# A kernel of two hybrid trunk layers on one core: S5 chunk states laid out by group instead of by chunk

## The chip, the cores and the metric

The kernel runs on one core of a Trainium2 chip. The metric is the time of one execution in microseconds (us) on the device. The engines of the core are named as in the profile: PE is the tensor engine's matmuls and PEld its weight loads (they overlap), DVE is VectorE, ACT is ScalarE, POOL is GpSimd, SP is the engine that issues nearly all DMAs.

## The reference, cut to what matters

Two layers run over 640 tokens (512 of a denoising request, 128 of a prompt) with 1024 channels. Each layer has a gated linear attention branch, a latent attention branch and an S5 branch, joined by gates. The change is in the S5 branch, a diagonal complex state space model over 32 groups with 64 states each, run forwards and backwards:

```
def complex_linear_scan(ab_re, ab_im, u_re, u_im, x0_re, x0_im):
    u_re = u_re.at[:, 0].add(ab_re * x0_re - ab_im * x0_im)
    u_im = u_im.at[:, 0].add(ab_re * x0_im + ab_im * x0_re)
    ...
    _, _, x_re, x_im = lax.associative_scan(combine, (a_re, a_im, u_re, u_im), axis=1)
    return x_re, x_im
...
    finals.append(jnp.stack([x_re[:, -1], x_im[:, -1]], axis=1))
    ...
    y_ssm = jnp.einsum('blgn,gpn->blgp', x_re, c_re) - jnp.einsum('blgn,gpn->blgp', x_im, c_im)
```

So for every group a state is carried from token to token (once in each direction), the output is a product of the states with a matrix per group, and the states after the prompt are themselves an output (`new_state_s5`).

## The kernel before, in words

The kernel cuts the 640 tokens into 80 chunks of 8. Per chunk and group it keeps one state per direction; the 128 partitions hold the 64 states' real and imaginary parts. These chunk states are X, one tile (named `mx` in the profile) of 128 partitions by 5248 elements of 4 bytes, with 164 chunk places times 32 groups: places 0 to 80 for the forward direction (`XZ[0]`), 82 to 161 for the backward one (`XZ[1]`), place 80 and 81 for the final states. Before the change the group is the last axis: the 32 groups of one chunk are neighbours, and the same group of the next chunk is 32 elements, 128 bytes, further.

Three stages of a layer work on X.

- `s5_z` (line 829) fills it: PE multiplies the chunk inputs `U` with a matrix per group and direction into PSUM, and ACT copies four groups by 80 chunks at a time into X (32 copies in all, through the helper on line 229).
- `s5_scan` (line 900) runs the recurrence on DVE. Fifteen steps treat 5 blocks of 16 chunks in both directions at once, 2 x 5 x 32 = 320 elements: five instructions each (lines 916 to 920), of which each reads or writes X once. Four single steps of 2 x 32 elements join the blocks. Then the DMAs of the final states leave (lines 930, 931). In a last part, for three blocks and two directions, four instructions of 15 x 32 = 480 elements (lines 951 to 954) add what came in from the block before; 951, 953 and 954 touch X, 952 takes a copy with changed sign that line 938 has made (96 elements).
- `s5_y` (line 957) makes the output on PE: for each group three matmuls with 80 columns of stationary operand, one with `U` (chunks are neighbours in it) and two with X (lines 972 to 975). A matmul of 4-byte operands shows as two pairs of weight load and matmul in the trace, so a group is six pairs. All matmuls are recorded under the helper's line 247.

What stands between these stages on PE is written out by hand: `fill(n)` takes n parts of projections that are wanted anyway. Each of the 24 turns of the scan is followed by `fill(4)`. A part is a contraction step of 128 channels, six pairs of load and matmul (four with the weight's rounded part `whi`, two with the rest `wlo`). Four parts share one half of a weight tile: SP loads it (`wraw`, line 268), ACT rounds it (`whi`, line 229), DVE subtracts (`wlo`, line 238), and each of the three has four buffers. The order on PE is the order of the program; on the other engines a scheduler sets a fixed order at build time, with the splits put between the scan's instructions.

Of the kernel before, what the change touches and what calls it, by code (L numbers as in the profile page):

```python
# [10 lines left out]
F32 = mybir.dt.float32  # L11
# [12 lines left out]
NC8 = 80  # L24
NB = 16
# [178 lines left out]
class Prog:  # L204
# [624 lines left out]
    def s5_z(self, p, fill):  # L829
        V = self.V  # L830

        X = self.mx().rearrange("p (c g) -> p c g", g=32)
        XZ = (X[:, 0:81], X[:, 82:162])
        sh = [128, 4, 8, 16]
        def front(b, d):
            r = p.tile([128, 4, 8, 16], F32, name="s5r", tag=f"s5r{d}", bufs=2 + d)
            tmp = p.tile([128, 4, 8, 16], F32, name="s5rtmp", tag=f"s5rtmp{d}", bufs=1)
            g = slice(32 * d + 4 * b, 32 * d + 4 * b + 4)
            w = [self.w[:, :, i, g].rearrange("p e g -> p g e") for i in range(2)]
            if d == 0:  # L840
                w = [x[:, :, ::-1] for x in w]
            self.outer(V, p, r, tmp, w[0], w[1], self.B1[:, 4 * b:4 * b + 4], self.B2[:, 4 * b:4 * b + 4], sh)
            ps = self.bank()
            for i in range(4):
                self.T.transpose(ps[:, 128 * i:128 * i + 128], r[:, i].rearrange("p a b -> p (a b)"), self.ident)
            pm = p.tile([128, 512], F32, name="s5pm", tag="s5pm", bufs=3)
            self.copy(pm, ps)
            return pm

        def back(b, d, pm):  # L850
            pz = self.bank()
            for i in range(4):
                self.mm(pz[:, NC8 * i:NC8 * i + NC8], pm[:, 128 * i:128 * i + 128], self.U[:, 4 * b + i, :])
            z = pz[:, 0:4 * NC8].rearrange("p (g c) -> p c g", g=4)
            gs = slice(4 * b, 4 * b + 4)
            if d == 0:
                self.copy(XZ[0][:, 1:81, gs], z)
            else:
                self.copy(XZ[1][:, 0:79, gs], z[:, 1:80])

        todo = []
        for n in range(16):
            todo.append((n // 2, n % 2, front(n // 2, n % 2)))
            if n:
                back(*todo.pop(0))
            fill(FILL[2])
        back(*todo.pop(0))
        x0 = self.vec("x0")
        V.tensor_copy(X[:, 81, :], XZ[1][:, 63, :])
        V.tensor_copy(XZ[0][:, 0, :], x0[:, 0:32])  # L870
        V.tensor_copy(XZ[1][:, 63, :], x0[:, 32:64])
        V.memset(XZ[0][:, 64, :], 0.0)
        V.memset(XZ[1][:, 79, :], 0.0)
        self.X, self.XZ = X, XZ

# [24 lines left out]
    def s5_scan(self, p):  # L900

        V = self.V
        X = self.X
        pt = self.pt.rearrange("p r e (d g) -> p r e d g", d=2)

        def at(f, b, n=1):

            a = X[:, f:82 + b + 1:82 + b - f, :]
            ps, ds, gs = a.ap
            return bass.AP(tensor=a.tensor, offset=a.offset, ap=[ps, ds, [NB * 32, n], gs])  # L910

        def step(prev, cur, e, n):
            ar, ai = (pt[:, r, e][:, :, None, :].to_broadcast([128, 2, n, 32]) for r in range(2))
            t1 = p.tile([128, 2, n, 32], F32, name="sc1", tag="sc1", bufs=2)
            t2 = p.tile([128, 2, n, 32], F32, name="sc2", tag="sc2", bufs=2)
            V.tensor_tensor(t1, prev, ar, op=ALU.mult)
            V.tensor_tensor(t2[0:64], prev[64:128], ai[64:128], op=ALU.mult)
            V.tensor_tensor(t2[64:128], prev[0:64], ai[0:64], op=ALU.mult)
            V.tensor_tensor(t1, t1, cur, op=ALU.add)
            V.tensor_tensor(cur, t1, t2, op=ALU.add)  # L920

        for i in range(1, NB):
            step(at(i - 1, NB - i, 5), at(i, NB - 1 - i, 5), 0, 5)
            yield
        step(at(79, 64), at(80, -1), 0, 1)
        for k in range(1, 4):
            step(at(NB * k - 1, 64 - NB * k), at(NB * k + NB - 1, 48 - NB * k), NB - 1, 1)
            yield
        o = self.o["s5o"][self.l]
        self.S.dma_start(o[:, 0:32], X[:, 80, :])  # L930
        self.S.dma_start(o[:, 32:64], X[:, 81, :])
        n = NB - 1
        sh = [128, n, 32]
        sw = p.tile([128, 2, 3, 32], F32, name="s5sw")
        for d in range(2):
            c = X[:, 15:48:16] if d == 0 else X[:, 98:131:16]
            for a, b in ((slice(0, 64), slice(64, 128)), (slice(64, 128), slice(0, 64))):
                V.tensor_scalar(sw[a, d], c[b], -1.0, None, op0=ALU.mult)
        for k in range(3):
            for d in range(2):  # L940
                t1 = p.tile(sh, F32, name="sf1", tag="sf1", bufs=2)
                t2 = p.tile(sh, F32, name="sf2", tag="sf2", bufs=2)
                if d == 0:
                    c = X[:, NB * k + 15]
                    x = X[:, NB * k + 16:NB * k + 16 + n]
                    w = [pt[:, r, 0:n, d] for r in range(2)]
                else:
                    c = X[:, 82 + NB * (k + 1)]
                    x = X[:, 82 + NB * k + 1:82 + NB * k + 16]
                    w = [pt[:, r, 0:n, d][:, ::-1] for r in range(2)]  # L950
                V.tensor_tensor(t1, w[0], c[:, None, :].to_broadcast(sh), op=ALU.mult)
                V.tensor_tensor(t2, w[1], sw[:, d, k][:, None, :].to_broadcast(sh), op=ALU.mult)
                V.tensor_tensor(x, x, t1, op=ALU.add)
                V.tensor_tensor(x, x, t2, op=ALU.add)
                yield
# [531 lines left out]
    def fill(self, n):  # L1487

        for _ in range(n):
            while self.stand:  # L1490
                try:
                    next(self.stand[0])
                    break
                except StopIteration:
                    self.stand.pop(0)
# [187 lines left out]
```

## Time and profile before

| | |
|---|---|
| median of 3 runs | 1574.49 us (1572.39 to 1583.06) |
| the profiled execution | 1574.24 us, span 1572.5 us |
| PE busy | 1506.5 us, 96% |
| DVE busy | 1054.3 us, 67% |
| ACT busy | 629.5 us, 40% |
| DMA, over the span | 182.09 MB, mean 116 GB/s |
| the 256 X pairs of `s5_y` | 46.1 us of matmul, 302 ns each (overlapping) |

The span is the time from the first to the last recorded instruction of the profiled execution. Busy time is what an engine spent in instructions; matmuls overlap, so that the distance of their starts says more than their duration. A row of a timeline gives the start, the time from the first start to the last end, the engine, line, operation, output and input with their shapes, and how many instructions in a row were merged. A row of grouped instructions gives after the bar the total in us and the mean in ns of one, and behind it the idle time ahead of them.

### The profile page before, as it was taken

The page shows a single profiled execution, that of the slowest core. Times are in us where ns is not written, and L with a number is a line of the kernel's source. Part 1 is how long each engine was busy: PE and PEld are TensorE (multiplying, and loading weights), DVE is VectorE, ACT ScalarE, POOL GpSimd, SP SyncE. Part 2 cuts the span into 40 slices and gives each one's busy share as a digit, 9 for nine tenths or more (in the row PEclk, how much of TensorE's full clock was granted, in tenths as well). Part 3 has the DMA queues.
Part 4 walks back from the last instruction along what each step waited for, and adds up shares of the span by engine and source line. Part 5 has one row for each costly group of instructions (what it writes and reads, how often), then busy time and mean ns, then how long its engine had stood idle before and what let it go on. Part 6 is the DMA issues. An engine that isn't in the chain of part 4 may idle for free. (4 is left out here: it accounts for less than half of the span.)

```text
span 1572.5 us, 28798 instructions
## 1 busy us (share of the span) xinstructions
PE 1506.5 (96%) x11334; PEld 1436.7 (91%) x11334; DVE 1054.3 (67%) x2435; ACT 629.5 (40%) x1171; POOL 46.5 (3%) x48
## 2 busy tenths in 40 slices
PE   5998999999999999999999899999999999999998
PEld 3788999988999888898998899999999999888998
DVE  8979694796556536879577579645766563487662
ACT  3324323555444454322324442254544442633321
POOL 0000000011000000000000000001300000000000
PEclk9998999999999999999999999999999999999999
DMA  9451435243312221237753333442331223212253
GB/s 347 158 151 49 122 113 167 90 133 102 103 63 75 85 75 56 78 110 241 258 195 99 97 79 113 138 133 87 115 114 61 74 81 111 69 55 68 91 169 104
DMA packets 109656, 182.09 MB, mean 116 GB/s; under 512 B 12752, under 2 KB 31120, under 8 KB 109520
## 3 DMA queue, kind: packets, MB, share of 16 engines
q1 hardware_dynamic: 109520, 180.25, 36.3%
q8 instruction: 89, 1.46, 0.4%
q14 instruction: 47, 0.39, 0.1%
HBM read 150.41 MB, written 29.79 MB: 115 GB/s over the span
## 5 line engine op out<-in xcount | busy, mean ns | idle before, releaser
L247 PE MATMUL pj<-h,whi 128*128 128x320 f32 x3456 | 664.8, 314 | 0.2 <-DVE og L488 0.2
L247 PEld LDWEIGHTS pj<-h,whi 128*128 128x128 f32 x3456 | 541.7, 189 | 6.5 <-issue 5.1
L229 ACT ACTIVATE whi<-wraw 128x512 fp32r<-128x512 f32 x326 | 204.9, 630 | 517.3 <-PE pj L247 384.1
L247 PE MATMUL pj<-h,wlo 128*128 128x320 f32 x1728 | 397.6, 310 | 0.0
L238 DVE TENSOR_TENSOR wlo<-wraw,whi 128x512 fp32r<-128x512 f32 x326 | 223.9, 688 | 216.5 <-ACT whi L229 209.8
L247 PEld LDWEIGHTS pj<-h,wlo 128*128 128x128 f32 x1728 | 290.8, 189 | 0.0
L247 PE MATMUL pj<-og,whi 128*128 128x320 f32 x736 | 142.9, 314 | 2.4 <-DVE og L238 2.4
L247 PEld LDWEIGHTS pj<-og,whi 128*128 128x128 f32 x736 | 115.4, 189 | 6.9 <-DVE og L238 3.2
L247 PE MATMUL pj<-whi,h 128*128 128x512 f32 x256 | 86.6, 400 | 5.1 <-ACT h L232 4.4
L247 PE MATMUL pj<-og,wlo 128*128 128x320 f32 x384 | 87.8, 310 | 0.0
L247 PEld LDWEIGHTS pj<-whi,h 128*128 128x128 f32 x256 | 48.8, 192 | 17.4 <-ACT h L232 5.0
L247 PEld LDWEIGHTS pj<-og,wlo 128*128 128x128 f32 x384 | 64.5, 188 | 0.0
L232 ACT ACTIVATE P<-bank,smx 128x384 f32<-128x384 f32 x64 | 36.5, 576 | 49.8 <-DVE smx L1235 49.8
L238 DVE TENSOR_TENSOR Ptl<-bank,Pth 128x512 fp32r<-128x512 f32 x48 | 31.7, 687 | 31.1 <-ACT Pth L229 30.9
L232 ACT ACTIVATE th<-pj 128x640 f32<-128x640 f32 x72 | 49.7, 690 | 6.3 <-PE pj L247 6.2
L247 PE MATMUL pj<-wlo,h 128*128 128x512 f32 x128 | 50.6, 396 | 0.0
L247 PE MATMUL pj<-s5g,whi 128*128 128x320 f32 x256 | 48.1, 310 | 0.0
L247 PE MATMUL bank<-s5qy,mx 128*80 128x128 f32 x256 | 46.1, 302 | 0.0
L577 DVE SCALAR_TENSOR_TENSOR mx<-pj,ada,tmp 128x320 f32<-128x320 f32 (+2 forms) x48 | 18.1, 433 | 39.6 <-PE pj L247 37.5
L1231 DVE TENSOR_REDUCE smx<-bank 128x1 f32<-128x384 f32 (+1 forms) x72 | 36.5, 524 | 10.6 <-PE bank L247 10.0
L229 ACT ACTIVATE Pth<-bank 128x512 fp32r<-128x512 f32 x48 | 27.1, 596 | 35.3 <-PE bank L1256 35.3
L1421 DVE SCALAR_TENSOR_TENSOR st<-st,bl,bank 64x128 f32<-64x128 f32 x112 | 38.8, 347 | 3.5
(349 smaller groups left out, 2320.2 us busy)
## 6 DMA issues: line engine op xcount, KB each, us to landing
wraw<-wpk SPq DMA_DIRECT2D x358, 256.0 KB, 2.8
og<-wpk SPq DMA_DIRECT2D x48, 256.0 KB, 5.4
qd<-s5qk SPq DMA_DIRECT2D x32, 256.0 KB, 2.9
s5qy<-qd SPq DMA_DIRECT2D x32, 256.0 KB, 4.0
gd<-gt SPq DMA_DIRECT2D x16, 320.0 KB, 2.8
gt<-gd SPq DMA_DIRECT2D x16, 320.0 KB, 3.1
md<-th SPq DMA_DIRECT2D x16, 320.0 KB, 2.3
th<-md SPq DMA_DIRECT2D x16, 320.0 KB, 3.5
```

Source lines behind the costliest of these rows:

```text
L229: self.A.activation(out, in_, AF.Copy, scale=scale)
L232: self.A.activation(out, in_, f, **kw)
L238: (eng or self.V).tensor_tensor(lo, src, hi.bitcast(F32), op=ALU.subtract)
L247: self.T.matmul(out, lhsT, rhs, start=start, stop=stop, skip_group_check=True, **kw)
L577: V.scalar_tensor_tensor(xn[:, j, lo:hi], ps[:, i, lo - 320 * i:hi - 320 * i], self.ads[l, 2][r][:, j:j + 1], xr[:, lo:hi], op0=ALU.mult, ...
L1231: V.tensor_reduce(mx[:, i:i + 1], ps[:, 0:w], axis=AX.X, op=ALU.max)
L1421: V.scalar_tensor_tensor(out, st[r, c, :], bl[r, c:c + 1], pu[c][r], op0=ALU.mult, op1=ALU.add)
```

## The change

X is laid out the other way round: the group is the outer axis and the 164 chunk places of a group are neighbours. The same chunk of the next group is 164 elements, 656 bytes, further. ACT's copies in `s5_z` go over groups outside and chunks inside. The scan keeps its order of dimensions (chunks outside, 32 groups inside). The final states are first copied into a small tile, and one DMA of 64 elements per partition takes the place of two of 32.

```diff
@@ s5_z
-        X = self.mx().rearrange("p (c g) -> p c g", g=32)
+        X = self.mx().rearrange("p (g c) -> p c g", g=32)
...
-            z = pz[:, 0:4 * NC8].rearrange("p (g c) -> p c g", g=4)
+            z = pz[:, 0:4 * NC8].rearrange("p (g c) -> p g c", g=4)
             gs = slice(4 * b, 4 * b + 4)
             if d == 0:
-                self.copy(XZ[0][:, 1:81, gs], z)
+                self.copy(XZ[0][:, 1:81, gs].rearrange("p c g -> p g c"), z)
             else:
-                self.copy(XZ[1][:, 0:79, gs], z[:, 1:80])
+                self.copy(XZ[1][:, 0:79, gs].rearrange("p c g -> p g c"), z[:, :, 1:80])
@@ s5_scan
-            return bass.AP(tensor=a.tensor, offset=a.offset, ap=[ps, ds, [NB * 32, n], gs])
+            return bass.AP(tensor=a.tensor, offset=a.offset, ap=[ps, ds, [NB, n], gs])
...
         o = self.o["s5o"][self.l]
-        self.S.dma_start(o[:, 0:32], X[:, 80, :])
-        self.S.dma_start(o[:, 32:64], X[:, 81, :])
+        xe = p.tile([128, 2, 32], F32, name="s5xe")
+        V.tensor_copy(xe, X[:, 80:82, :])
+        self.S.dma_start(o, xe.rearrange("p d g -> p (d g)"))
```

On DVE the order of the instructions stays. This is the place in layer 0 where the four single steps meet the last part of the scan (`sc` and `sf` are the scan's temporaries, `s5pt` the powers of the transition, `wlo` a weight split, `gt` a gate); - is before, + is the change:

```order
@@ -432,11 +432,12 @@
 L919 TENSOR_TENSOR sc_2542<-sc_2542,mx 128x64
 L918 TENSOR_TENSOR sc_2550<-mx,s5pt 64x64
-L951 TENSOR_TENSOR sf_2672<-s5pt,mx 128x480
+L952 TENSOR_TENSOR sf_2673<-s5pt,mx 128x480
 L238 TENSOR_TENSOR wlo<-wraw,whi 128x512
 L919 TENSOR_TENSOR sc_2549<-sc_2549,mx 128x64
-L920 TENSOR_TENSOR mx<-sc_2542,sc_2543 128x64
+L920 TENSOR_TENSOR mx<-sc_2542,sc_2543 128x2x32
 L488 SCALAR_TENSOR_TENSOR gt<-th,pj 128x640
-L953 TENSOR_TENSOR mx<-mx,sf_2672 128x480
+L954 TENSOR_TENSOR mx<-mx,sf_2673 128x15x32
 L920 TENSOR_TENSOR mx<-sc_2549,sc_2550 128x2x32
+L931 COPY s5xe<-mx 128x64
 L238 TENSOR_TENSOR wlo<-wraw,whi 128x512
```

Only the copy is new; the shapes show that the 480 elements of X are no longer one run, and the lines behind the new one have moved by one.

On SP's queue this is the place of the final states in layer 0 (`gd` is a store of a gate, `wraw` a raw weight load); first before:

```order
70 L1062 DMA gd_104<-gt 128x640
71 L268 DMA wraw<-wpk 128x512 x2
72 L930 DMA s5o<-mx 128x32
73 L931 DMA s5o<-mx 128x32
74 L1062 DMA gd_104<-gt 128x640
75 L268 DMA wraw<-wpk 128x512 x2
```

and with the change:

```order
70 L1063 DMA gd_104<-gt 128x640
71 L268 DMA wraw<-wpk 128x512 x2
72 L1063 DMA gd_104<-gt 128x640
73 L932 DMA s5o<-s5xe 128x64
74 L268 DMA wraw<-wpk 128x512 x2
75 L1063 DMA gd_104<-gt 128x640
```

The one DMA that is left stands behind one gate store more than the two did. PE's and ACT's order is unchanged, and so is the order of everything else on DVE and SP, but that in layer 1 the one DMA of final states also stands one place from where the two did.

## Rows read from the trace of the kernel before

**Rows 1.** Page, busy us by engine, share of the span, instructions.

```profile
PE 1506.5 (96%) x11334; PEld 1436.7 (91%) x11334; DVE 1054.3 (67%) x2435; ACT 629.5 (40%) x1171; POOL 46.5 (3%) x48
```

**Rows 2.** Stretches: length, busy us (instructions) by engine, PE clock, DMA share, GB/s.

```profile
170.00:246.10 76.10, 76.10 (x521) 76.05 (x520) 73.50 (x154) 20.01 (x32) 0.00 (x0) 1.00 0.44 134
...
931.00:1004.20 73.20, 73.20 (x501) 73.20 (x500) 70.64 (x151) 19.58 (x32) 0.00 (x0) 1.00 0.42 126
```

**Rows 3.** Timeline of PE in s5_y, layer 0: start, us, what.

```profile
254.71 0.38 PE L247 MATMUL bank<-s5m,s5u 128*80 128x128 f32 x2
254.93 0.72 PE L247 MATMUL bank<-s5qy,mx 128*80 128x128 f32 x4
255.49 0.38 PE L247 MATMUL bank<-s5m,s5u 128*80 128x128 f32 x2
255.70 0.72 PE L247 MATMUL bank<-s5qy,mx 128*80 128x128 f32 x4
...
260.14 0.38 PE L247 MATMUL bank<-s5m,s5u 128*80 128x128 f32 x2
...
261.80 0.75 PE L984 MATMUL bank<-c,s5yb 80*128 80x80 f32 x8
262.34 0.83 PE L247 MATMUL pj<-h,whi 128*128 128x320 f32 x4
```

**Rows 4.** Groups of DVE instructions by shape: total us, mean ns; idle before.

```profile
L549 DVE TENSOR_TENSOR mx<-mx,tmp 128x640 f32<-128x640 f32 x32 | 26.2, 818 | 0.1
...
L916 DVE TENSOR_TENSOR sc<-mx,s5pt 128x320 f32<-128x320 f32 x30 | 14.7, 490 | 0.9
...
L920 DVE TENSOR_TENSOR mx<-sc,sc 128x320 f32<-128x320 f32 x30 | 14.7, 489 | 0.6
...
L954 DVE TENSOR_TENSOR mx<-mx,sf 128x480 f32<-128x480 f32 x12 | 7.6, 649 | 0.0
...
L938 DVE TENSOR_SCALAR s5sw<-mx 64x96 f32<-64x96 f32 x8 | 2.0, 248 | 0.1
...
L916 DVE TENSOR_TENSOR sc<-mx,s5pt 128x64 f32<-128x64 f32 x8 | 1.8, 222 | 0.1
```

**Rows 5.** Groups of ACT instructions by shape, as above.

```profile
L229 ACT ACTIVATE mx<-bank 128x320 f32<-128x320 f32 x16 | 7.0, 438 | 4.1 <-PE bank L247 4.1
...
L229 ACT ACTIVATE s5u<-bank 128x320 f32<-128x320 f32 x16 | 6.1, 432 | 4.0 <-PE bank L824 4.0
```

**Rows 6.** Timeline of ACT, the last halves rounded in layer 0's scan.

```profile
243.18 0.63 ACT L229 ACTIVATE whi<-wraw 128x512 fp32r<-128x512 f32 x1 [2.30 <-PE pj L247]
```

**Rows 7.** Timeline of DVE, the end of the scan in layer 0.

```profile
244.81 1.22 DVE L954 TENSOR_TENSOR mx<-mx,sf 128x480 f32<-128x480 f32 x2
245.94 0.68 DVE L238 TENSOR_TENSOR wlo<-wraw,whi 128x512 fp32r<-128x512 f32 x1
```

**Rows 8.** Timeline of PE, the last projections ahead of s5_y, layer 0.

```profile
253.83 0.75 PE L247 MATMUL pj<-h,whi 128*128 128x320 f32 x4
254.42 0.46 PE L247 MATMUL pj<-h,wlo 128*128 128x320 f32 x2
```

**Rows 9.** Timeline of DVE, the end of the scan in layer 1.

```profile
1002.95 0.68 DVE L238 TENSOR_TENSOR wlo<-wraw,whi 128x512 fp32r<-128x512 f32 x1
1003.55 0.64 DVE L954 TENSOR_TENSOR mx<-mx,sf 128x480 f32<-128x480 f32 x1
```

**Rows 10.** Timeline of PE, projections ahead of s5_y, layer 1.

```profile
1012.14 0.46 PE L247 MATMUL pj<-h,wlo 128*128 128x320 f32 x2
```

**Rows 11.** Stretches ahead of and in s5_z, layer 0, columns as in rows 2.

```profile
120.00:130.00 10.00, 4.57 (x38) 4.07 (x36) 7.10 (x13) 4.59 (x9) 0.00 (x0) 0.80 0.35 111
130.00:140.00 10.00, 8.31 (x50) 8.29 (x51) 10.00 (x18) 2.66 (x5) 0.00 (x0) 0.68 0.01 2
```

**Rows 12.** Timeline of PE there, behind a wait for DVE.

```profile
132.43 1.42 PE L247 MATMUL pj<-h,whi 128*128 128x320 f32 x4
...
134.18 1.05 PE L845 MATMUL bank<-c,s5r 128*128 128x128 f32 x4
```

## Prediction

> **What bounds the kernel now.** I began with busy time by engine: the tensor engine (PE) is busy for 96% of the span, VectorE (DVE) for 67% [rows 1]. A microsecond taken from PE's own work is therefore nearly a microsecond of the run, and DVE work costs nothing as long as PE doesn't wait for it. But 67% is a mean over stages, so the next view is busy time by stretch, around the lines that the diff touches. The S5 scan runs at 170 to 246 us in layer 0 and at 931 to 1004 us in layer 1, and in both DVE is busy for 96.6% of the time (73.50 of 76.10 us, 70.64 of 73.20 us) while PE is never idle [rows 2]. PE works there on projections (the `fill` calls), whose weights DVE has to split, in the same queue as the scan's instructions. So there are two full engines side by side, and the change touches both: it shortens something on PE in the output stage that follows (`s5_y`), and it changes the address pattern of almost everything that DVE does in the scan.
>
> **What it gives PE.** In `s5_y` a group of channels takes six pairs of weight load and matmul: two with the input `U` as stationary operand, four with the chunk states X. Each pair has 128 moving columns and a stationary operand of 80 columns. The two U pairs take 0.22 or 0.21 us together, so 0.1075 us a pair; from group to group it is (260.14 - 254.71) / 7 = 0.776 us [rows 3]. The four X pairs thus take 0.56 us, 0.140 us a pair. The only difference between the operands is the step from column to column: 4 bytes in U, 128 bytes in X. After the change X has 4 bytes too, so I give its pairs U's price: six pairs of 0.1075 us are 0.645 us, and 0.131 us is saved per group. With 32 groups in each of two layers that is 64 x 0.131 = **8.4 us off PE**. The lower bound is nothing, if the extra 0.03 us a pair is not the load's; U's pairs, of the same shape, speak against that. PE's order of instructions is the same as before, so nothing else moves there.
>
> **What it costs DVE.** The neighbours in X are now the chunks, but the scan still runs over 32 groups inside and chunks outside, so each of its accesses to X has an innermost step of 164 elements, 656 bytes, where it had 4 bytes. The elements touched in a layer: in the 15 steps, five instructions of 320 (L916 to L920, 30 each in two layers); in the four single steps, five of 64; in the last part 18 of 480 (L951, L953 and L954, 12 each in two layers; L952 doesn't touch X); and the sign flips, four of 96 [rows 4]. That is 24,000 + 1,280 + 8,640 + 384; with five small fills and copies of 32 and the new copy of 64, 34,528 elements.
>
> No DVE instruction of before reads or writes with such a step, so its price has to be bounded. Below: nothing. ScalarE's copies into X read PSUM with a step of 320 bytes and take 438 ns, against 432 ns for the copy of as many elements into U, which reads neighbours [rows 5]. So a long step can be free, on another engine and from PSUM. The nearest row for the same memory is PE's: a column 128 bytes from the last one costs 0.140 us / 80 = 1.75 ns, while eight loads of 128 neighbouring columns with their transposes take 262.34 - 261.80 = 0.54 us, at most 0.53 ns a column [rows 3]. DVE needs (818 - 490) ns / 320 = 1.025 ns per neighbouring element (640 against 320 elements) [rows 4]. If an element on a line of its own takes DVE as long as PE, the extra is 0.725 ns; if DVE needs a second beat, which is what an engine with a beat of 1.025 ns does when 1.75 ns don't fit into one, it is 1.025 ns. I take the second beat, since the scan's memory is the one of PE's row and not that of ScalarE's, and keep 0 and 0.725 ns for the range.
>
> [...]
>
> With the second beat a layer's scan grows by 34,528 x 1.025 ns = 35.4 us, and the new copy adds about 0.2 us at its old price (a 64-element instruction takes 222 ns [rows 4]): **E = 35.6 us per layer**.
>
> **How much of E is hidden.** DVE's order is also the same as before, apart from the new copy in either layer: the weight splits (`wlo`) stand between the same scan instructions. DVE has no idle time that could take E, so a split late in the stage comes later by all of it. What hides is PE's lead. Four buffers of split weights go round; one half lasts PE four times the 0.88 us between 253.83 [rows 8] and 254.71 [rows 3], 3.52 us, and the half whose first part is written at 243.18 [rows 6] is used three halves later, at 253.83. Its `wlo` is ready at 245.94 + 0.68 = 246.62 [rows 7] and wanted at 254.42 [rows 8]: a lead of 7.8 us. The scan itself ends at 244.81 + 1.22 = 246.03 [rows 7], and the first X pair is at 254.93 [rows 3], a lead of 8.9 us; the split decides. In layer 1 the last split inside the scan ends at 1003.63, ahead of the scan's last instruction (0.64 us, of which about 0.5 us is its share of E) [rows 9], and is wanted at 1012.14 [rows 10]: 8.5 + 0.5 = 9.0 us. So PE waits (35.6 - 7.8) + (35.6 - 9.0) = 27.8 + 26.6 = **54.4 us**. The waits can't be made up, because PE has no idle time afterwards in which it would have been waiting for something else.
>
> The edits left: ScalarE's 32 copies into X now write neighbours and read neighbours; by [rows 5] that is at most 6 ns each, off the path. On SP's queue two DMAs of final states become one, which waits for the new DVE copy; behind it stand gate stores and weight loads. The copy sits right behind the instruction for which the old DMAs waited, so the wait is the copy's own 0.3 us or so, and the four raw weight buffers cover it; if they didn't, PE would wait 0.3 us per layer. I count nothing.
>
> **The sum.** Against the profiled run's own 1574.24 us (span 1572.5 us and 1.7 us around it; the median of the runs shown is 1574.49 us): 1574.24 - 8.4 + 54.4 = 1620.2 us. The change breaks even where 2E - 16.8 = 8.4 us, that is E = 12.6 us, an extra of 0.36 ns per element.
>
> **The rivals.**
> *The step is dearer for PE than free, but less than a second beat.* With 0.725 ns, E = 25.2 us, the waits are 33.6 us, the time is 1599.4 us. If reads pay the second beat and writes are free (L920 and the small writes, some 5,100 elements, drop out), E = 30.4 us and the time is 1609.8 us. [...]
> *The step is free for DVE.* Then E is the new copy's 0.2 us, far under the 7.8 us of lead; PE waits for nothing, and the time is 1574.24 - 8.4 = 1565.8 us. This is the case on the other side; it decides for every extra under 0.36 ns an element. ScalarE's copies speak for it, PE's loads against.
> *Dearer still.* L953 and L954 read and write X in one instruction; if both ends pay apart, 12 x 480 x 1.025 ns = 5.9 us more per layer gives 1632 us. [...]
> *The change doesn't do what it says:* X's loads stay dear for another reason, and the scan slows all the same: 1628 us.
>
> **How the numbers follow.** Second beat 0.48; between free and second beat, 0.20; dearer still 0.10; loads unchanged 0.04; free 0.18. The likeliest gives **1620 us**. The range from 1592 to 1645 us takes in everything but "free" and a far tail, so about 8 in 10. A measurement here tells about 1% from no change, 16 us: "free" (0.5% faster) is within it. Slower by over 1%: 0.80; within 1%: 0.18; faster by over 1%: 0.02, for which PE would have to gain twice what its rows allow.
>
> **What would show it.** Right: L916 to L920 at about 490 + 328 = 820 ns for 320 elements and L954 at about 1,140 ns; PE waiting for `wlo` or X inside the scan stages, some 27 us in each; X pairs in `s5_y` at U's 0.1075 us. Wrong: scan instructions still at 490 ns with PE at 100% through the scan, and a span shorter by 8 us. Slow scan instructions without waits of PE would mean that I misjudged the lead.

## The result and the profile after

The changed kernel takes 1616.86 us (median of six runs, 1614.26 to 1619.62) against 1574.82 us for the kernel before, measured beside it: a ratio of 1.0258, with a 95% interval of 1.0232 to 1.0285. The profiled execution took 1619.62 us, 1617.8 us of it span. The forecast was 1620.0 us in a range of 1592 to 1645 us, "slower" with 0.80. So the time is as forecast; but two terms of the sum, the length of the scan and the part of it that is hidden, are wrong by a quarter and more, and their errors cancel.

Busy time by engine on the page after (columns as in [rows 1]), and the two scan stages (as in [rows 2]; the stretches hold the DVE instructions of those of before and the new copy):

```profile
PE 1517.0 (94%) x11334; PEld 1444.3 (89%) x11334; DVE 1107.0 (68%) x2437; ACT 630.0 (39%) x1171; POOL 46.4 (3%) x48
```

```profile
169.18:271.97 102.79, 87.43 (x537) 85.83 (x537) 100.19 (x155) 21.25 (x34) 0.00 (x0) 0.90 0.33 102
955.89:1055.30 99.41, 82.06 (x526) 80.10 (x525) 96.88 (x152) 20.18 (x33) 0.00 (x0) 0.93 0.31 93
```

VectorE (DVE) gained 52.7 us of busy time, all of it in these two stages (26.7 and 26.2 us): they last 102.8 and 99.4 us where they lasted 76.1 and 73.2 us, and DVE is busy for 97% of them. The tensor engine (PE), which never paused there, is idle for 102.79 - 87.43 = 15.4 us in layer 0, and its pairs of load and matmul take 87.43 us / 537 = 0.163 us each in place of 76.10 us / 521 = 0.146 us, at a mean granted clock of 0.90.

The groups of DVE instructions by shape that answer to [rows 4] (line 955 is line 954 of before, 939 is 938; line 953, which doesn't touch X, is there for comparison):

```profile
L920 DVE TENSOR_TENSOR mx<-sc,sc 128x320 f32<-128x320 f32 x30 | 22.4, 745 | 0.6
L916 DVE TENSOR_TENSOR sc<-mx,s5pt 128x320 f32<-128x320 f32 x30 | 22.2, 741 | 0.9
L955 DVE TENSOR_TENSOR mx<-mx,sf 128x480 f32<-128x480 f32 x12 | 12.5, 1060 | 0.0
L953 DVE TENSOR_TENSOR sf<-s5pt,s5sw 128x480 f32<-128x480 f32 x12 | 7.8, 669 | 0.0
L939 DVE TENSOR_SCALAR s5sw<-mx 64x96 f32<-64x96 f32 x8 | 2.6, 323 | 0.1
L916 DVE TENSOR_TENSOR sc<-mx,s5pt 128x64 f32<-128x64 f32 x8 | 2.2, 269 | 0.1
```

320 elements went from 490 to 741 or 745 ns, that is 0.79 ns more per element; 480 elements from 649 to 1060 ns, 0.86 ns; 64 from 222 to 269 ns, 0.73 ns; 96 from 248 to 323 ns, 0.78 ns. With the numbers of elements of the prediction: 24,000 x 0.79 + 8,640 x 0.86 + 1,280 x 0.73 + 384 x 0.78 ns + 0.2 us = 27.8 us per layer, not 35.6 us. Neighbouring instructions overlap a little (the L955 that starts at 263.02 us lasts 1.07 us, and the next instruction starts at 263.96 us), so the distance says more: from the start of its first instruction to the end of its last, the scan takes 102.4 us in place of 75.7 us in layer 0 and 98.7 us in place of 72.5 us in layer 1, that is 26.7 and 26.2 us more, as DVE's busy time has it.

What PE waited for, in all (us in total, times, longest; the list goes on with waits that were there before):

```profile
PE pj L247 <- DVE misc L1056: 15.7, 2, 9.0
PE pj L247 <- DVE gt L488: 14.4, 9, 3.7
...
PE pj L247 <- DVE wlo L238: 3.0, 3, 1.3
```

33 us of new waits, and only 3 us of them for the weight splits (`wlo`) that the prediction named. The others are for lines 488 and 1056. These are DVE's evacuations, the instructions that empty a `pj` tile: the gate (`gt`), and an addition into `misc`. PE writes its projections into two `pj` tiles in PSUM in turn, so a projection can't start before DVE has read out the last but one.

S5_y, the timeline of PE in layer 0 (start, us, what; answers to [rows 3]):

```profile
278.12 0.38 PE L247 MATMUL bank<-s5m,s5u 128*80 128x128 f32 x2
278.34 0.60 PE L247 MATMUL bank<-s5qy,mx 128*80 128x128 f32 x4
...
282.71 0.38 PE L247 MATMUL bank<-s5m,s5u 128*80 128x128 f32 x2
```

Seven groups take 282.71 - 278.12 = 4.59 us, 0.656 us each in place of 0.776 us. The first X pair stands at 278.34 us, 23.4 us later than before; as this scan began 0.8 us earlier, 24.2 us were lost from the scan's start to s5_y. In layer 1 the same stretch (from the scan's first instruction, 931.66 before and 956.55 after, to the first X pair, 1016.17 and 1064.37) grew by 23.3 us. The s5_y stages, from the first X pair to the end of the last, got shorter by 3.5 and 3.9 us. 24.2 + 23.3 - 7.4 = 40.1 us of the 45.3 us between the two spans. Of the other 5 us, 1.5 us in each layer are matmuls behind s5_y at a lower clock (0.62 as the mean of 326 to 330 us in layer 0). This spell comes and goes from one execution to the next: of the runs below five have it in one layer and the others in none, with waits in the scan or without. The last 2 us lie scattered between the stages, where the run with the states alone (below) differs from before by 3.6 us with no change there.

### The profile page after: what moved, and what is told of

Read it like the earlier page. It is cut to its first block, busy times and chain, and to the rows that moved or that the text cites. A ratio compares the mean times of both kernels' runs of the same rounds, so it can differ in the third digit from the quotient of the medians.

```text
span 1617.8 us, 28792 instructions
## 1 busy us (share of the span) xinstructions
PE 1517.0 (94%) x11334; PEld 1444.3 (89%) x11334; DVE 1107.0 (68%) x2437; ACT 630.0 (39%) x1171; POOL 46.4 (3%) x48
## 5 line engine op out<-in xcount | busy, mean ns | idle before, releaser
L247 PE MATMUL pj<-h,whi 128*128 128x320 f32 x3456 | 675.8, 317 | 30.3 <-DVE misc L1056 15.7
L247 PEld LDWEIGHTS pj<-h,whi 128*128 128x128 f32 x3456 | 550.5, 192 | 39.7 <-issue 34.9
L247 PE MATMUL pj<-h,wlo 128*128 128x320 f32 x1728 | 402.1, 313 | 3.0 <-DVE wlo L238 3.0
L247 PEld LDWEIGHTS pj<-h,wlo 128*128 128x128 f32 x1728 | 294.8, 191 | 3.8 <-DVE wlo L238 3.8
L247 PEld LDWEIGHTS pj<-whi,h 128*128 128x128 f32 x256 | 48.7, 191 | 18.6 <-ACT h L232 6.3
L247 PEld LDWEIGHTS pj<-s5g,whi 128*128 128x128 f32 x256 | 42.2, 197 | 0.0
```

Of the source, the lines that this page charges most:

```text
L247: self.T.matmul(out, lhsT, rhs, start=start, stop=stop, skip_group_check=True, **kw)
```

## The fixed order, seen between two gates

DVE's timeline from one gate to the next, before:

```profile
208.13 0.82 DVE L488 SCALAR_TENSOR_TENSOR gt<-th,pj 128x640 f32<-128x640 f32 x1
...
210.92 0.69 DVE L238 TENSOR_TENSOR wlo<-wraw,whi 128x512 fp32r<-128x512 f32 x1
...
215.12 0.82 DVE L488 SCALAR_TENSOR_TENSOR gt<-th,pj 128x640 f32<-128x640 f32 x1
```

and after:

```profile
221.93 0.81 DVE L488 SCALAR_TENSOR_TENSOR gt<-th,pj 128x640 f32<-128x640 f32 x1
...
225.74 0.69 DVE L238 TENSOR_TENSOR wlo<-wraw,whi 128x512 fp32r<-128x512 f32 x1
...
231.47 0.81 DVE L488 SCALAR_TENSOR_TENSOR gt<-th,pj 128x640 f32<-128x640 f32 x1
```

In both there are ten scan instructions, two splits and the gate, in the same order. Before, this takes 215.12 - 208.13 = 6.99 us. One projection takes PE eight times 0.88 us, 7.04 us: here the order fits PE's pace exactly and leaves no slack. After, it takes 231.47 - 221.93 = 9.54 us, 2.55 us more, and the next projection but one has to wait for it. The longest wait is for the first such evacuation, which has 39 scan instructions ahead of it since the scan's start in layer 0 (63 in layer 1, where the wait is 9.0 us). Layer 0, DVE, then PE; the bracket is the wait:

```profile
202.46 0.82 DVE L1056 TENSOR_TENSOR misc<-pj,misc 32x640 fp32r<-32x640 f32 x1
```

```profile
203.43 1.40 PE L247 MATMUL pj<-h,whi 128*128 128x320 f32 x4 [6.68 <-DVE misc L1056]
...
205.16 1.27 PE L247 MATMUL pj<-h,whi 128*128 128x320 f32 x4
```

After 6.68 us without work the next six pairs take 205.16 - 203.43 = 1.73 us in place of 0.88 us: the granted clock is 0.52 as the mean of 200 to 210 us. That is why the sum of the waits is smaller than the loss: the rest is PE working slowly, ahead of its next wait.

## The experiments

Ratios are to the kernel before, run beside each of them, with 95% intervals.

**A price list.** Behind the last layer of the kernel before, such lines as

```diff
+    V.tensor_tensor(d(), src[:, 0:1280:4], C, op=ALU.mult)  # read step 4
+    V.tensor_tensor(W[:, 0:10, :], X[:, 0:10, :], C3, op=ALU.mult)  # read and write step 164
```

> The kernel before, and behind its last layer a list of single operations that belong to no result: fp32 multiplications and copies of 320 elements per partition on VectorE with the elements of one operand 1, 2, 3, 4, 8, 16 or 164 floats apart (read, written, or both), copies of 640 elements on ScalarE with a step of 32 floats on either side, two operations on GpSimd, and groups of 16 matmuls whose 80-column stationary operand is 1 to 64 floats apart. It asks whether the step alone is what made the scan's instructions longer (490 to 741 ns for 320 elements). Theory (the step alone): about 490 ns at step 1 and about 740 ns at step 164, for a read as for a write and for both together, and a bend at some step between; a matmul pair that gets shorter from step 32 to step 1 by about 79 + 29 ns, as in the changed kernel. Rival (the scan's own surroundings made it longer, by ScalarE or PE using the same memory at that time): 490 ns at every step when nothing else runs. Rival (each strided operand costs by itself): 740 ns for one strided operand, about 990 ns for two. The total time says nothing here but that some 50 us stand behind the last layer.

DVE's groups (lines 1667 to 1673: read steps of 1, 2, 3, 4, 8, 16 and 164 floats; 1674: pairs of neighbours, eight floats from pair to pair; 1675 to 1678: writes with steps of 2, 4, 16 and 164; 1679: one read and the write with 164; 1680: both reads):

```profile
L1667 DVE TENSOR_TENSOR pdst<-mx,pcon 128x320 f32<-128x320 f32 x1 | 0.5, 484 | 0.0
L1668 DVE TENSOR_TENSOR pdst<-mx,pcon 128x320 f32<-128x320 f32 x1 | 0.5, 485 | 0.0
L1669 DVE TENSOR_TENSOR pdst<-mx,pcon 128x320 f32<-128x320 f32 x1 | 0.6, 581 | 0.0
L1670 DVE TENSOR_TENSOR pdst<-mx,pcon 128x320 f32<-128x320 f32 x1 | 0.7, 721 | 0.0
...
L1673 DVE TENSOR_TENSOR pdst<-mx,pcon 128x320 f32<-128x320 f32 x1 | 0.7, 720 | 0.0
L1674 DVE TENSOR_TENSOR pdst<-mx,pcon 128x320 f32<-128x320 f32 x1 | 0.5, 497 | 0.0
L1675 DVE TENSOR_TENSOR pwide<-pcon 128x320 f32<-128x320 f32 x1 | 0.5, 486 | 0.0
...
L1678 DVE TENSOR_TENSOR pwide<-pcon 128x320 f32<-128x320 f32 x1 | 0.7, 747 | 0.0
L1679 DVE TENSOR_TENSOR pwide<-mx,pcon 128x320 f32<-128x320 f32 x1 | 0.8, 751 | 0.0
L1680 DVE TENSOR_TENSOR pdst<-mx 128x320 f32<-128x320 f32 x1 | 0.7, 735 | 0.0
```

The step alone does it, with no scan around it. The cost bends between 2 floats (485 ns, free) and 4 (721 ns), and stays there up to 164 (720 ns). A write pays as a read does (747 and 720 ns at 164 floats), and two strided operands cost no more than one (735 and 751 ns): that rival is out. So is the surroundings' share: ScalarE did nothing meanwhile, and PE's loads, which ran beside the whole list, ran beside the steps of 1 and 2 floats too. In bytes of the step it is 485 ns at 8, 581 ns at 12 and 721 ns at 16; what sets the place of the bend no run shows.

PE's weight loads in the same list, with steps of 1, 2, 4 and 32 floats (each row from a stretch inside the 32 loads of that step):

```profile
L247 PEld LDWEIGHTS bank<-pcon,mx 128*80 128x80 f32 x11 | 1.2, 150 | 0.0
L247 PEld LDWEIGHTS bank<-pcon,mx 128*80 128x80 f32 x23 | 2.6, 153 | 0.0
L247 PEld LDWEIGHTS bank<-pcon,mx 128*80 128x80 f32 x29 | 4.3, 243 | 0.0
L247 PEld LDWEIGHTS bank<-pcon,mx 128*80 128x80 f32 x26 | 3.7, 233 | 0.0
```

So PE's loads bend at the same place: 8 bytes are nearly free (153 against 150 ns), 16 bytes have the whole price (243 ns, against 233 ns at 128 bytes).

**PE's side alone.** S5_y loads 80 neighbours of X, which are other states than those that the reference takes there; the amount of work is the same, and the scan is that of before:

```diff
-                    self.mm(o, self.XZ[d][:, 0:NC8, g], q[d][:, i],
+                    self.mm(o, self.flat[:, 162 * g + 81 * d:162 * g + 81 * d + NC8], q[d][:, i],
```

> The kernel before, whose s5_y loads 80 neighbouring columns of X for each of its 64 groups in place of 80 columns 128 bytes apart: the matrix that it takes is another one than the reference's (other states), the number of matmuls, loads, columns and waits is the same. Only TensorE's side of the change is in it. Theory: the two s5_y stages get shorter by 3.5 and 3.9 us, the sum 7.4 us, so 1574.2 - 7.4 = about 1567 us, a ratio of 0.995, and the group at 0.65 to 0.66 us. The prediction's own term says -8.4 us, 1566 us. Rival (the shorter group came from VectorE or ScalarE, which are less in its way in the changed kernel): no change, 1574.

Measured: 0.9951 (0.9935 to 0.9966), 7.7 us off. All 256 X matmuls have the changed kernel's 273 ns, where before has 302 ns. The gain is the load's.

```profile
L247 PE MATMUL bank<-s5qy,mx 128*80 128x128 f32 x256 | 38.4, 273 | 0.0
```

**The final states alone.**

```diff
-        self.S.dma_start(o[:, 0:32], X[:, 80, :])
-        self.S.dma_start(o[:, 32:64], X[:, 81, :])
+        xe = p.tile([128, 2, 32], F32, name="s5xe")
+        V.tensor_copy(xe, X[:, 80:82, :])
+        self.S.dma_start(o, xe.rearrange("p d g -> p (d g)"))
```

> The kernel before with one part of the change alone: the two final states are copied into a small tile by VectorE and written out by one transfer in place of two. X keeps its layout. Theory: one copy of 64 elements (0.1 to 0.2 us) in each layer on VectorE, one DMA issue less on SyncE, and nobody waits for either: 1575 us, a ratio of 0.999 to 1.001. Rival (the copy or the later issue is what costs some of the 42 us): a ratio over 1.002.

Measured: 0.9994 (0.9980 to 1.0008). This part costs nothing that can be measured.

**VectorE's length alone, in the layout of before.** Only the scan's scratch tiles are strided (and have one buffer in place of two, by which the last part of the scan gets another order on DVE):

```diff
-            t1 = p.tile([128, 2, n, 32], F32, name="sc1", tag="sc1", bufs=2)
+            t1, t2 = (p.tile([128, 2, n, 32, 4], F32, name=f"sc{i}", tag=f"sc{i}", bufs=1)[:, :, :, :, 0] for i in (1, 2))
```

> The kernel before with X laid out as before (groups as neighbours, TensorE's loads 128 bytes apart as before), in which only the scan's scratch tiles (sc1, sc2, sf1, sf2) have their elements four floats apart. The price list gave 712 to 741 ns for a 320-element multiplication with one operand four floats apart, and 735 to 751 ns with two, against 484 ns with none. TensorE's order of instructions is that of before. Theory (the length of the scan's instructions on VectorE is all that counts, wherever it comes from; X's layout itself is innocent): the scan's own instructions take 27 to 28 us more in each layer as in the changed kernel, TensorE waits some 24 us in each layer in the lines of the gate and misc, and the time is 1574 + 47 to 52 = 1621 to 1626 us, a ratio of 1.030 to 1.033. Rival (X with a step of 656 bytes is what disturbs TensorE or ScalarE): VectorE's instructions longer, but clearly less than +40 us. Rival (the prediction's lead of 7.8 and 9.0 us): 1574 + 38 = 1612 us.

Measured: 1.0308 (1.0294 to 1.0322). DVE's groups (its lines 919 and 952 are 920 and 954 of before) and PE's waits:

```profile
L919 DVE TENSOR_TENSOR mx<-sc,sc 128x320 f32<-128x320 f32 x30 | 22.0, 734 | 0.6
...
L952 DVE TENSOR_TENSOR mx<-mx,sf 128x480 f32<-128x480 f32 x12 | 12.3, 1023 | 0.2
```

```profile
PE pj L247 <- DVE misc L1053: 15.5, 2, 9.1
PE pj L247 <- DVE gt L488: 15.1, 10, 3.4
```

X is untouched, PE's order is that of before, and the loss is the changed kernel's with the same two waits: 22.3 and 24.4 us from the scan's start to s5_y, against 24.2 and 23.3 us. The sum closes too: the changed kernel's 1.0258 and the 0.0049 that PE's side gave make 1.0307, and this run has 1.0308. That it is so close is partly chance, since these scans grew by 28.1 and 28.9 us (all four instructions of the last part are strided here).

**The same length, made of more instructions.** Scan instructions are done twice, all with neighbours:

```diff
+            if n > 1:
+                V.tensor_tensor(t1, prev, ar, op=ALU.mult)
+                V.tensor_tensor(t2[0:64], prev[64:128], ai[64:128], op=ALU.mult)
```

> The kernel before, with its layout and neighbouring accesses, in which some of the scan's multiplications are done twice into the same tile with the same values: about 26.5 us more of VectorE in each of the two scans, spread along it as the changed kernel's longer instructions are. Nothing is strided and TensorE's loads stay. Theory (VectorE's time alone makes the wait, through the tiles in PSUM that it must empty, and only 2 to 3 us of it in each layer are hidden): TensorE waits for the gate and misc lines of VectorE, 23 to 25 us in each layer with the slower clock, about 1574.2 + 48 = 1622 us. The prediction's lead (7.8 and 9.0 us, by the weight splits): 1574.2 + 53 - 16.8 = about 1610 us, and waits on the tile wlo. Rival (the strided accesses disturb the other engines, and the time of VectorE is not what counts): far less than +40 us.

Measured: 1.0247 (1.0219 to 1.0274), +39 us: between the two sums. PE's timeline at s5_y says why:

```profile
274.69 1.29 PE L247 MATMUL bank<-s5qy,mx 128*80 128x128 f32 x4 [16.98 <-DVE mx L961]
```

The order of DVE was made anew for the added instructions: from the second one on, most evacuations still have 9 to 16 scan instructions ahead of them, and 32 stand behind the last gate. So PE does all its projections at its own pace and then waits once, 17 us, for X. DVE's busy time grew by 25.1 us a layer, and s5_y began 19.9 and 19.4 us later after the scan's start, so 5 to 6 us are hidden in each layer. S5_y itself begins at a granted clock of 0.50 (274.7 to 278.7 us), and is 2.1 and 2.3 us longer than before. The time of DVE alone makes a wait, but its place and part of its size come from the order. How much less the changed kernel would lose in such an order was not measured: no run has its accesses in another order, and none gives PE a third `pj` tile.

**Evacuations first.**

```diff
-        self.V.scalar_tensor_tensor(self.v2(g), self.v2(th), 1.0, ps, op0=ALU.add, op1=ALU.mult)
+        with self.tc.high_priority(4000):
+            self.V.scalar_tensor_tensor(self.v2(g), self.v2(th), 1.0, ps, op0=ALU.add, op1=ALU.mult)
```

> The changed kernel, in which VectorE's instructions that empty TensorE's two PSUM tiles (the gate of line 488 and the addition of line 1056) are given a higher priority, so that they stand further ahead in VectorE's order. The work is the same. Theory (TensorE's wait comes through these two tiles, and only 2 to 3 us per layer are hidden by them): the waits on the gate and misc lines shrink, those on the weight split (wlo) take their place, and the lead grows towards the 7.8 and 9.0 us that the prediction read off the splits: up to 6 us per layer less than the changed kernel, so 1605 to 1612 us against 1617. Rival (the prediction: the weight split is what TensorE waits for): no change, 1617 us, since the splits come no earlier. Rival (VectorE's time in the scan is simply longer than TensorE's work, whatever the order within it): no change in the sum either, with the wait moved to another line.

Measured: 1.0244 (1.0218 to 1.0269). The raised priority moved no instruction on PE, DVE or ScalarE, so this is a second measurement of the changed kernel and tells nothing of the order.

**More standing work in the scan.** `FILL[3]`, the number of parts of projections (units) behind each turn of the scan, is 5 and 6 in place of 4:

```diff
-FILL = (17, 2, 1, 4, 1, 4, 10, 1, 7, 1)
+FILL = (17, 2, 1, 5, 1, 4, 10, 1, 7, 1)
```

> The changed kernel, in which the scan's stage is given five units of standing work after each step of the scan in place of four: about 24 units more for TensorE in each layer, taken from the stages behind it. Theory (the stage is VectorE's: it is busy 97.5 of 100.1 us there, TensorE's 84.6 us of work up to the first load of X has to wait; of the standing work a unit costs TensorE about 0.87 us and VectorE a fifth of that): the stage holds about 105 us of TensorE's work beside about 105 us of VectorE's, the wait of some 24 us in each layer falls below 8 us, and the time to about 1580 to 1590 us. Rival (TensorE waits for the order in which VectorE empties its two PSUM tiles and not for VectorE's sum): each unit more brings its own wait, and the time stays at 1610 to 1620 us. Rival (the units are missing later on): the wait moves behind s5_y, again 1610 to 1620 us, with other lines waited for.

> As the run with five units, with six: about 48 units, 42 us of TensorE's work, more in the scan's stage of each layer than in the changed kernel. Theory (the stage is VectorE's): the stage holds about 126 us of TensorE's work beside about 110 us of VectorE's, TensorE is the bound again, nearly all the wait is gone, and the gain of s5_y's loads (7.4 us) shows: 1567 to 1580 us, at or under the kernel before. Rival (order of the PSUM tiles): 1610 to 1620 us. Rival (the standing work runs out, and the later stages that lived on it wait): between 1580 and 1620 us with the wait behind s5_y.

Measured: 1.0416 (1.0402 to 1.0429) and 1.0542 (1.0527 to 1.0557): worse by 24 and 45 us than the changed kernel, against every expectation. DVE and PE with five units:

```profile
271.44 2.05 DVE L955 TENSOR_TENSOR mx<-mx,sf 128x480 f32<-128x480 f32 x2
```

```profile
301.07 0.60 PE L247 MATMUL bank<-s5qy,mx 128*80 128x128 f32 x4
```

The scan ends at 273.5 us and takes 102.2 us, as in the changed kernel (102.4 us, to 271.9 us), and the evacuations stand behind as many scan instructions as there; the new units stand behind the scan, and s5_y begins 27.6 us after its end in place of 6.4 us (48.7 us with six). So the waits in the scan are all still there, and of the 42 us of work that were moved ahead, 24 us were not won back further on. What the later stages lack is not settled: part of it shows as 10 us of waits on ScalarE's `P`.

**The splits on GpSimd.**

```diff
+                        self.lo = self.G
                         fill(FILL[3])
...
-            self.split(hi, lo, r)
+            self.split(hi, lo, r, self.lo)
```

> The changed kernel, in which the weight splits (wlo) of the standing work that runs beside the scan are computed by GpSimd in place of VectorE: 24 in each layer, 0.69 us each, 16.5 us of VectorE. The rest of VectorE's order and TensorE's order stay as they are. GpSimd took 955 ns for a multiplication of 320 elements, so about 1.5 us for a split of 512, against 3.5 us of TensorE's work for each. Theory (the scan's stage is bound by the sum of VectorE's work, 97.5 of 100.1 us, and hides only VectorE's 2.6 us of idle time; whatever is taken from that sum comes back): the scan gets shorter by about 16 us in each layer, the wait falls from 24 to about 8 us, and the time is 1617 - 33 = about 1584 us (1580 to 1590). Rival (TensorE waits for the two PSUM tiles in VectorE's fixed order, whatever the sum): little change, 1605 to 1617 us. Rival (the prediction's lead, by the splits): with the splits off VectorE the wait is gone altogether, 1565 to 1575 us. Rival (GpSimd and VectorE get in each other's way): VectorE's instructions longer, 1600 us or more.

Measured: 1.0447 (1.0428 to 1.0467), 31 us worse than the changed kernel, where my theory of VectorE's sum had 33 us of gain. A group of DVE's, GpSimd's in the first scan, one subtraction of GpSimd and the DVE instruction beside it, and PE's waits in the first scan:

```profile
L920 DVE TENSOR_TENSOR mx<-sc,sc 128x320 f32<-128x320 f32 x30 | 30.2, 1006 | 1.0
```

```profile
L238 POOL TENSOR_TENSOR wlo<-wraw,whi 128x512 fp32r<-128x512 f32 x22 | 33.5, 1521 | 94.7 <-ACT whi L229 82.9 <-PE bank L845 7.5 <-DMA wraw<-wpk 4.3
```

```profile
177.58 1.45 POOL L238 TENSOR_TENSOR wlo<-wraw,whi 128x512 fp32r<-128x512 f32 x1 [3.16 <-ACT whi L229]
177.90 1.74 DVE L920 TENSOR_TENSOR mx<-sc,sc 128x320 f32<-128x320 f32 x1
```

```profile
PE pj L247 <- DVE gt L488: 16.2, 4, 7.8
PE pj L247 <- DVE misc L1056: 15.1, 1, 15.1
```

Two things went against it. GpSimd's subtractions stopped the scan: an instruction of 320 elements that began during one ended 0.5 to 0.6 us after it and took 1.5 to 1.8 us, while the others took their 0.71 to 0.77 us (the mean of 1006 ns at line 920 mixes the two). That is 15 us in each layer, nearly what the splits had taken. And the order didn't stay, though the expectation had it so: with the splits gone, 44 scan instructions in place of 39 stood ahead of the first evacuation, then 11, 14, 19 and 23 where there had been 10, 10, 10 and 16. The evacuations came later, and PE waited 15.1 us at once. So the rival "GpSimd and VectorE get in each other's way" (1600 us or more) was right; the rival "fixed order" named the waits but had 1605 to 1617 us, since it took the order as staying. DVE's part of the scan got only 3 us longer in layer 0 (105.4 us), while s5_y began 14.5 us later after the scan's start: so the sum of VectorE's work alone doesn't set the wait.

**The gain without the loss.** The kernel before, with X copied for s5_y by ScalarE (a), with a unit of standing work moved in front of the transposes (b, `FILL[4]` from 1 to 0, `FILL[9]` from 1 to 2), and with every second copy on GpSimd (c):

```diff
+            x2 = p.tile([128, 2, 4, NC8], F32, name="x2", tag="x2", bufs=2)
+            for d in range(2):
+                self.copy(x2[:, d], self.XZ[d][:, 0:NC8, 4 * b:4 * b + 4].rearrange("p c g -> p g c"))
...
-                    self.mm(o, self.XZ[d][:, 0:NC8, g], q[d][:, i],
+                    self.mm(o, x2[:, d, i], q[d][:, i],
```

> The kernel before with its layout for the scan, and a second small tile into which ScalarE copies X, four groups at a time (32 copies of 320 elements in each layer), with the chunks as neighbours; s5_y loads from that. The tile yb has one buffer in place of two. ScalarE took 1302 ns for 640 elements read with a step of 32 floats, so about 650 ns for each copy, 10.4 us in each layer on an engine that is busy 39% of the span; four groups take TensorE 2.6 us, two copies 1.3 us. Theory (the load step alone gives the gain, the scan's accesses alone the loss): TensorE's groups at 0.656 us, 7.4 us in all as in the run with TensorE's side alone, so 1567 us, a ratio of 0.995, if ScalarE keeps ahead. Rival (the copies come late on ScalarE, behind the weight copies, or hold these up): between 1570 and 1590 us with waits on x2 or whi.

> The run with ScalarE's copies of X (its gain of 3.8 us in each layer was given back by three waits of 1.3 us for s5yb at the transposes, since ScalarE had copies of X ahead of the copy into s5yb), with the unit of standing work that stood behind s5_m moved to stand in front of the transposes, so that TensorE has 0.87 us more to do while ScalarE gets there. Theory: the three waits fall to some 0.4 us each, and 5 to 6 us of the 7.4 us gain show: about 1569 us, a ratio of 0.996. Rival (s5_m is then late, as its own cover is gone): a ratio of 1.000 or more, with waits on s5m.

> The run with ScalarE's copies of X, with every second copy (direction 1) on GpSimd, which is idle there. ScalarE then has one copy of 0.75 us for each four groups in place of two; GpSimd took 612 ns for a contiguous copy of 320 elements, the strided one may take up to 1.2 us, against 2.6 us of TensorE's work for four groups. Theory: ScalarE reaches s5yb 0.75 to 1.5 us sooner, the waits at the transposes go, and the gain of s5_y's loads shows: 1567 to 1569 us, a ratio of 0.995 to 0.996. Rival (GpSimd's copy is late or slows VectorE): waits on x2 by GpSimd, a ratio of 1.000 or more.

Measured: (a) 1.0001 (0.9989 to 1.0014), (b) 0.9996 (0.9983 to 1.0010), (c) 0.9973 (0.9960 to 0.9986). ScalarE and PE in (a), layer 0:

```profile
261.33 1.42 ACT L229 ACTIVATE x<-mx 128x320 f32<-128x320 f32 x2 [0.72 <-PE bank L247]
262.65 0.58 ACT L229 ACTIVATE s5yb<-bank 80x512 f32<-80x512 f32 x1
```

```profile
263.28 0.77 PE L987 MATMUL bank<-c,s5yb 80*128 80x80 f32 x8 [1.18 <-ACT s5yb L229]
```

The groups of (a) have their 0.656 us, 3.8 us off in each layer; three transposes wait 1.2 us each (3.5 us) for a copy that stands behind two copies of X in ScalarE's queue. In (c) there is one copy ahead, three waits make 1.9 us, and the 0.3% that are left, some 4 us, are measured: it is the fastest here of the kernels that take the reference's states, but by little. Why (b), whose s5_y stages are 2.4 us shorter each, shows so little in the whole is open: in its profiled execution about as much is lost between the two layers' S5 branches (1.5 us of it the spell at the lower clock), a stretch that the states alone changed by 3.6 us too, and the difference is of the size of the interval.

## Why the prediction came out right

- **PE's gain, 8.4 us: right in kind, 1 us too large.** 0.656 us per group in place of 0.645 us; 7.4 us by the stages, 7.7 us by the run with PE's side alone. That U's and X's loads differ by their step and nothing else was shown by that run and by the price list.
- **The price of the step, 1.025 ns: mis-sized.** It measured 0.79 to 0.86 ns. That an element with a long step takes DVE a whole second beat was my estimate, and no run shows such a beat; the bound worked out from PE's loads, 0.725 ns, was the nearer one. E was 27.8 us by the sum of the prediction, 26.7 and 26.2 us by the scan's whole length, not 35.6 us. That read and write in one instruction don't pay twice was right (751 ns against 720 and 747 ns), as was the number of elements.
- **The lead, 7.8 and 9.0 us: mis-sized, and the step that failed is "the split decides".** I compared two things that PE takes from DVE, the splits and X, and left out the third: DVE must empty the two `pj` tiles. Of the 26.7 and 26.2 us, 24.2 and 23.3 us were waited for or worked off at the lower clock, so 2.5 and 2.9 us were hidden. The trace of before had the smaller lead too. The next two rows of it are the gate at the end of the scan in layer 0 and the projection that needs the emptied tile:

```profile
244.07 0.81 DVE L488 SCALAR_TENSOR_TENSOR gt<-th,pj 128x640 f32<-128x640 f32 x1
```

```profile
246.79 0.75 PE L247 MATMUL pj<-h,whi 128*128 128x320 f32 x4
```

  The gate ends at 244.88 us, so this lead is 1.9 us, far from 7.8 us. The corresponding rows after have PE waiting for just that:

```profile
269.10 0.89 DVE L488 SCALAR_TENSOR_TENSOR gt<-th,pj 128x640 f32<-128x640 f32 x1
```

```profile
270.14 0.82 PE L247 MATMUL pj<-h,whi 128*128 128x320 f32 x4 [0.55 <-DVE gt L488]
```

  With this lead the loss comes out in both layers. Counted from the scan's start, this gate ends 100.5 us after it in place of 74.5 us (269.99 - 169.53 and 244.88 - 170.35); 25.9 us less the lead of 1.9 us are 24.0 us, and 24.2 us were lost. The last gate that PE waits for in layer 1 comes 26.2 us later and had a lead of 3.1 us (1004.92 to 1008.03 us before): 23.1 us, and 23.3 us were lost.
- **The sum.** With the measured 26.7 and 26.2 us and the predicted leads the waits would have been 18.9 + 17.2 = 36.1 us and the time 1574.2 - 7.4 + 36.1 = 1602.9 us; with the predicted E and the measured 2.5 and 2.9 us hidden, 1574.2 - 7.4 + 33.1 + 32.7 = 1632.6 us. That 1620 us came out of both errors together was luck. In the list of signs, the loss in each scan (24 and 23 us, forecast 27 us of waits) nearly held; its line (`wlo` or X) did not.
- **The clock.** The granted clock was low around the longest waits: 0.52 as the mean of 200 to 210 us, with the wait of 6.68 us, and 0.50 from 1005 to 1015 us, with the one of 9.0 us; before has a stretch at 0.68 behind a wait [rows 11], with six pairs in 1.75 us [rows 12]. While DVE sets the pace this is mostly hidden: the two gates account for the loss to 0.2 us, and no run shows a price of the return to the full clock (1.00) on top of that. PE's low clock costs time where the wait stands right ahead of s5_y and DVE no longer sets the pace: in the run with more instructions, at 0.50, 2.1 and 2.3 us. The spell behind s5_y (1.5 us in each layer) is not shown to come from the waits: the run with the evacuations first, which is the same kernel, has it in layer 1 only, the runs with five and six units, which wait as much in the scan, don't have it, and run (c), which has no wait in the scan, has it in layer 1.
- **The final states** cost nothing, as forecast.

## To carry to other kernels

Before a layout is turned for one engine, write down the innermost step in bytes that every other engine gets from it: here one engine gained 3.8 us a layer from a step of 4 bytes, and the other lost some 27 us from a step of 656. For what a longer instruction costs, list everything that the waiting engine takes from that queue, the emptying of its PSUM tiles too, and take the smallest lead of all. A queue whose order was made for short instructions kept that order here when they got longer; more work to run beside them, or less work in the queue, need not help: here neither did.

## What was not expected of the hardware

- VectorE's 32-bit multiplications of 320 elements pay for the step in a bend, not in proportion: 485 ns at 8 bytes, 581 at 12, 712 to 751 from 16 up; pairs of neighbours were nearly free at the one distance tried (497 ns at 32 bytes from pair to pair).
- A VectorE copy of 320 elements took 341 ns with neighbours, 442 ns written with 656 bytes and 948 ns read with 656 bytes. The last is not shown to be the step's price: GpSimd's multiplication of the list ran until 0.64 us into it, and the copy ended 0.31 us after that. ScalarE's copies of 640 elements within SBUF took 737 ns, and 1302 to 1357 ns with 128 bytes on either side or both, though its copies of 320 elements out of PSUM with a step of 320 bytes were nearly free (438 against 432 ns [rows 5]).
- GpSimd's subtractions of 512 elements (1521 ns) held up the scan's instruction that began beside them: with 320 elements it took 1.5 to 1.8 us in place of 0.74 us and ended 0.5 to 0.6 us after the subtraction. A gate, which reads one operand from PSUM, took its usual 0.82 us though it began beside one (at 284.15 us).
- PE's weight load of 80 columns took 150 ns at a step of 4 bytes, 153 ns at 8, 243 ns at 16 and 233 ns at 128 bytes: the price is not in the distance here either, and it bends where VectorE's does.
